# A first stage with twelve channel tiles as float32 products in place of six split ones

## The chip, the cores and the metric

The kernel runs on one core of one Trainium2 chip. The metric is the device time of one execution in microseconds (us); lower is better.

## The reference, cut to what matters

Two blocks follow each other on 256 tokens of 1024 channels, all in float32. The change lies at the start of the first block:

```
shift, scale, gate = adaln(c, w_ada_mix, b_ada_mix)      # silu(c) @ w + b, cut in three
h = rms_norm(x, norm_mix_w) * (1 + scale) + shift
p = h @ w_in                                             # [256, 1024] x [1024, 9248]
a, b = p[:, 0:1024], p[:, 1024:2048]                     # gated input of the convolution branch
u = a * sigmoid(b)                                       # then a causal convolution of 31 taps, a layer
                                                         # norm over the channels, silu, @ w_conv_out
z, xBC, dt, gates = the other columns of p               # state space branch
x = x + gate * (merged branches @ w_out)
```

After it come the feed-forward of the first block and a second block with two mixers (gated delta rule, gated linear attention) and two MLPs. They are not changed.

## The kernel before

Tokens are two tiles of 128. Nearly every weight goes through `w3`: a DMA into a buffer `raw` (six of them), a cast `whi` by ACT and the rest `wlo = raw - whi` by DVE, both in float32r. `whi` and `wlo` share eight buffers, tag "w". A product then is three float32r matmuls (`mm3`, L185 to L187): whi·hi, whi·lo, wlo·hi of the activations `hh`, `hl`. For some items `wlo` is made by a DMA with addition instead (L166, issued by POOL): those with a running number over `NW` that four doesn't divide. The order of the instructions on each engine, and of the DMAs on SP's queue, is written ahead by the program's scheduler from priorities; on the chip each engine follows it and waits where an operand is late.

`start()` makes h. For each k of the eight blocks of 128 input channels it loads two items of `w_ada_mix`, multiplies and sums them against silu(c) on DVE (L399; `g`, that is `self.sc`, holds silu(c) on every partition), adds biases, transposes block k of the normed x (L312), scales and shifts it into `f` (L323), and splits f into `hh` and `hl`. Beside this it already multiplies six channel tiles (three of a, three of b) by item k of `w_abe`, 768 columns. Their six accumulators, [128, 256] each, take half a PSUM bank each: three banks of tag "a", three of tag "b".

`state_space()` turns the three finished pairs into u (`ev_ab`: tanh on ACT L572, product on DVE L573) and starts their convolution taps (`conv_taps`, L490: 30 dependent DVE instructions for each of eight channel tiles, at a priority far behind all else, so that they fill DVE's gaps), then multiplies dt (`small_tok`), the other five pairs from `w_ab` (two items each), B and C (`w_bc`), and the groups of the state space part. `mix_gates` and `merge` follow. In `merge` four pairs i of `w_ssm_out` are multiplied; before the last of them stands `conv_ln`, the layer norm over the channels of the convolution's result `acc`, which makes the operands `ch` and `cl` of the `w_conv_out` products. The first of these products needs all 240 taps.

## Time and profile before

| | us |
|---|---|
| three runs | 1447.05, 1451.47, 1452.64 |
| their median | 1451.47 |
| span of the profiled execution, first to last instruction | 1448.5 |
| PE busy in the span | 1317.5 (91%) |
| DVE busy | 991.1 (68%) |
| ACT busy | 755.5 (52%) |

The profile gives the span of its execution and no separate time for it; the span lies 2.97 us under the median of the three runs. PE is TensorE's matmuls, PEld its weight loads, DVE VectorE, ACT ScalarE, POOL GpSimd, SPq the issuing of DMAs by SyncE. Times in rows are us from the span's start. A matmul's busy time includes its way through the array, so the time that one costs in a dense run is read from start to start.

### The profile page before, as it was taken

To read this page: it belongs to the slowest core of one execution; us is meant where nothing else is said; L and a number is where in the kernel's file an instruction comes from. 1 tells how busy PE (TensorE), PEld (TensorE's weight loads), DVE (VectorE), ACT (ScalarE), POOL (GpSimd) and SP (SyncE) were. 2 spreads that over 40 slices of the span, in tenths; PEclk is the share of its full clock that TensorE was granted. 3 is DMA by queue.
4 is the path that set the end of the run, shared out by engine and by line. 5 is a ranking of instruction groups with operands and counts; after the bars stand their busy time and mean duration, and the time that the engine had idled before them with its cause. 6 is when DMAs were issued, how large, how long until landed. Compare 5 with 4: busy or idle time off the path is not lost. (4 is left out here: it accounts for less than half of the span.)

```text
span 1448.5 us, 21890 instructions
## 1 busy us (share of the span) xinstructions
PE 1317.5 (91%) x8408; PEld 1183.6 (82%) x8408; DVE 991.1 (68%) x1797; ACT 755.5 (52%) x1202; POOL 162.1 (11%) x179
## 2 busy tenths in 40 slices
PE   5899999979999999988768878999998998999997
PEld 4888788879987999978767866799886986788896
DVE  7878898669567664734579975855464796765453
ACT  4667687635446443626695434544443645454350
POOL 0112232210000000012411431000000000000000
PEclk9999999999999999999879999999998999999999
DMA  9899789998266764739468214765354313576430
GB/s 338 280 266 262 193 232 237 289 290 310 83 214 210 248 213 162 252 124 238 108 155 209 88 45 145 256 206 187 136 189 144 117 59 117 173 252 213 156 123 29
DMA packets 75049, 273.33 MB, mean 189 GB/s; under 512 B 8608, under 2 KB 8736, under 8 KB 74433
## 3 DMA queue, kind: packets, MB, share of 16 engines
q1 hardware_dynamic: 62208, 224.08, 44.7%
q0 software_dynamic: 12736, 47.85, 15.9%
q8 instruction: 66, 1.08, 0.3%
q14 instruction: 39, 0.31, 0.1%
HBM read 232.06 MB, written 2.10 MB: 162 GB/s over the span
## 5 line engine op out<-in xcount | busy, mean ns | idle before, releaser
L187 PE MATMUL psa<-hh,wlo 128*128 128x256 f32 x1448 | 420.3, 290 | 24.1 <-DMA wlo<-raw 20.7
L185 PE MATMUL psa<-hh,whi 128*128 128x256 f32 x1448 | 419.6, 290 | 3.7 <-DVE c L490 1.8
L186 PE MATMUL psa<-hl,whi 128*128 128x256 f32 x1448 | 418.0, 289 | 0.8 <-DVE hl L180 0.5
L170 DVE TENSOR_TENSOR wlo<-raw,whi 128x1024 fp32r<-128x1024 f32 (+1 forms) x203 | 244.5, 1211 | 155.3 <-ACT whi L169 148.8
L169 ACT CAST whi<-raw 128x1024 fp32r<-128x1024 f32 (+1 forms) x203 | 210.1, 1040 | 215.0 <-PE psa L186 143.8
L187 PEld LDWEIGHTS psa<-hh,wlo 128*128 128x128 f32 x1448 | 284.5, 196 | 30.7 <-DMA wlo<-raw 25.1
L185 PEld LDWEIGHTS psa<-hh,whi 128*128 128x128 f32 x1448 | 284.9, 197 | 8.0 <-ACT hh L179 2.9
L186 PEld LDWEIGHTS psa<-hl,whi 128*128 128x128 f32 x1448 | 284.3, 196 | 4.0 <-DVE hl L180 1.8
L170 DVE TENSOR_TENSOR xlo<-raw,xhi 128x1024 fp32r<-128x1024 f32 x100 | 121.0, 1221 | 60.9 <-ACT xhi L169 57.1
L169 ACT CAST xhi<-raw 128x1024 fp32r<-128x1024 f32 x100 | 104.8, 1050 | 93.7 <-DMA raw<-in_w_mlp 58.1
L185 PE MATMUL psb<-xhi,hid 128*128 128x512 f32 x344 | 136.1, 395 | 1.6 <-ACT hid L316 1.6
L187 PE MATMUL psb<-xhi,hidl 128*128 128x512 f32 x344 | 136.1, 396 | 0.0
L186 PE MATMUL psb<-xlo,hid 128*128 128x512 f32 x344 | 135.7, 395 | 0.0
L166 POOL DMA_DIRECT2D wlo<-raw x72 | 62.7, 871 | 419.5 <-ACT wlo L165 194.5
L490 DVE SCALAR_TENSOR_TENSOR acc<-u,vecs,acc 128x229 f32<-128x229 f32 (+28 forms) x240 | 105.1, 479 | 0.3
L165 ACT ACTIVATE wlo<-raw 128x1024 fp32r<-128x1024 f32 x72 | 76.2, 1058 | 43.7 <-PE psa L186 30.0
L186 PE MATMUL psa<-wlo,hh 128*128 128x512 f32 x208 | 83.9, 405 | 4.1 <-DVE wlo L170 3.2
L185 PE MATMUL psa<-whi,hh 128*128 128x512 f32 x208 | 85.0, 410 | 1.0 <-ACT hh L179 0.8
L399 DVE CUSTOM_DVE_ANT_0 raw<-raw,g 128x1024 f32<-128x1024 f32 x48 | 58.6, 1220 | 38.8 <-DMA raw<-in_w_ada_ffn 21.6
L187 PE MATMUL psa<-whi,hl 128*128 128x512 f32 x208 | 83.5, 404 | 0.0
L185 PEld LDWEIGHTS psb<-xhi,hid 128*128 128x128 f32 x344 | 64.8, 188 | 15.6 <-ACT hid L316 1.8
L187 PEld LDWEIGHTS psb<-xhi,hidl 128*128 128x128 f32 x344 | 64.7, 188 | 15.0
(388 smaller groups left out, 2234.7 us busy)
## 6 DMA issues: line engine op xcount, KB each, us to landing
raw<-in_w_mlp SPq DMA_DIRECT2D x120, 512.0 KB, 4.1
wlo<-raw POOLq DMA_DIRECT2D x72, 512.0 KB, 7.4
raw<-in_w_ffn_in SPq DMA_DIRECT2D x40, 512.0 KB, 4.3
raw<-in_w_ada_mix SPq DMA_DIRECT2D x24, 512.0 KB, 5.5
raw<-in_w_ada_ffn SPq DMA_DIRECT2D x24, 512.0 KB, 5.1
raw<-in_w_qkv SPq DMA_DIRECT2D x24, 512.0 KB, 5.9
raw<-in_w_ffn_down SPq DMA_DIRECT2D x22, 512.0 KB, 4.3
raw<-in_w_xs SPq DMA_DIRECT2D x16, 512.0 KB, 4.9
```

The lines of the kernel that those rows point to most:

```text
L165: nc.scalar.activation(out=lo, in_=t, func=AF.Copy, scale=-1.0)
L166: nc.gpsimd.dma_start(out=lo, in_=t, accum_op=ALU.add)
L169: nc.scalar.copy(hi, t)
L170: nc.vector.tensor_tensor(out=lo, in0=t, in1=hi.bitcast(F32), op=ALU.subtract)
L185: mm(out, ah, bh, start=start, stop=False)
L186: mm(out, ah, bl, start=False, stop=False)
L187: mm(out, al, bh, start=False, stop=stop)
L399: self.nc.vector.tensor_tensor_reduce(out=w, in0=w, in1=self.sc, scale=1.0, scalar=0.0, op0=ALU.mult, op1=ALU.add, accum_out=mod[:, i : i ...
L490: nc.vector.scalar_tensor_tensor(out=o, in0=i, scalar=taps[:, j : j + 1], in1=o, op0=ALU.mult, op1=ALU.add)
```

## The change

- c is loaded as [128, 8] (`c8`, 4 KB) and not as a broadcast [128, 1024]. Its silu is taken on eight columns, and `rows_of`, the former body of `gate_rows`, spreads it over the partitions: eight diagonal matrices on DVE, eight products with a matrix of ones on TensorE, two copies by ACT. The identity's load moves ahead of x's.
- The first stage makes twelve channel tiles (`NE = 6` pairs). Their weights are used as they arrive, in float32, without a split: one float32 matmul in place of three float32r ones. They are loaded straight into the buffers of tag "w", two pieces of 128 x 768 for each k. Two accumulators share a bank; only the first product of a bank has `start`.
- f of both tiles of tokens is one [128, 256] operand, scaled by one instruction, and is split by one pair of instructions behind the products.
- Two pairs instead of five are left for `w_ab`. The running number is set so that the items from `w_bc` on are split as before.
- The masks' load on POOL's queue keeps its place in the program, behind the first stage. `gate_rows` takes one buffer of tag "f" for four diagonals.

```diff
-NW = 14
+NW = 15
+NE = 6
 def consts(self):
-        self.sc = self.g4()
-        t = self.smt([P, D], "xn")
-        nc.sync.dma_start(self.sc, self.A["c"].broadcast_to([P, D]))
-        nc.scalar.activation(out=t, in_=self.sc, func=AF.Tanh, scale=0.5)
+        self.mod2 = cp.tile([P, 24], F32, name="mod2")
+        self.c8 = self.mod2[:, 0:8]
+        nc.sync.dma_start(self.c8, self.A["c8"])
+        nc.sync.dma_start(self.ident, self.A["masks"][:, 0])
+    def silu_c(self):
+        t = self.mod2[:, 8:16]
+        nc.scalar.activation(out=t, in_=self.c8, func=AF.Tanh, scale=0.5)
         nc.vector.tensor_scalar(out=t, in0=t, scalar1=0.5, scalar2=0.5, op0=ALU.mult, op1=ALU.add)
-        nc.vector.tensor_tensor(out=self.sc, in0=t, in1=self.sc, op=ALU.mult)
+        nc.vector.tensor_tensor(out=t, in0=t, in1=self.c8, op=ALU.mult)
+        self.sc = self.rows_of(t, 1.0)
 def load_consts(self):
-        nc.gpsimd.dma_start(self.mk, self.A["masks"][:, 1:NMASK0])
+        self.tc.keep_in_program_order(nc.gpsimd.dma_start(self.mk, self.A["masks"][:, 1:NMASK0]))
     def gate_rows(self, mod, scale):
+        return self.rows_of(mod[:, 16:24], scale)
+    def rows_of(self, v, scale):
         g = self.g4()
         for hf in range(2):
             b = self.pS()
+            dgs = self.smt([P, 4, P], "f")
             for k4 in range(4):
                 k = hf * 4 + k4
-                dg = self.smt([P, P], "dg")
+                dg = dgs[:, k4]
                 nc.vector.tensor_scalar(
-                    out=dg, in0=self.ident, scalar1=mod[:, 16 + k : 17 + k], scalar2=scale, op0=ALU.mult, op1=ALU.mult
+                    out=dg, in0=self.ident, scalar1=v[:, k : k + 1], scalar2=scale, op0=ALU.mult, op1=ALU.mult
                 )
                 nc.tensor.matmul(b[:, k4 * P : (k4 + 1) * P], self.ones, dg, start=True, stop=True)
             nc.scalar.copy(g[:, hf * 512 : hf * 512 + 512], b)
 def start(self):
-        nc.sync.dma_start(self.ident, A["masks"][:, 0])
+        self.silu_c()
-        banks = [(self.pa(), self.pb()) for i in range(3)]
+        banks = [self.pa() if i % 2 == 0 else self.pb() for i in range(NE)]
         for k in range(8):
...
+            b = self.pS()[:, :T]
             for t in range(2):
-                self.xpose_split(xn[t], t, h[0], h[1], a, mod[:, 0:8], ks=(k,), n=1)
-            wh, wl = self.w3("w_abe", k, 6)
-            for i in range(3):
-                for m in range(2):
-                    self.mm3(
-                        banks[i][m][:, :T], wh[:, 2 * i + m], wl[:, 2 * i + m], h[0][:, :, k], h[1][:, :, k],
-                        k == 0, k == 7,
-                    )
+                nc.tensor.transpose(b[:, t * P : (t + 1) * P], xn[t][:, k * P : (k + 1) * P], self.ident)
+            f = self.smt([P, 4, P], "f").rearrange("p t c -> p (t c)")[:, :T]
+            nc.scalar.activation(out=f, in_=b, func=AF.Identity, scale=a[:, k : k + 1], bias=mod[:, k : k + 1])
+            for e in range(2):
+                w = self.wp.tile([P, 1024], F32, tag="w", bufs=8, name=self.nm("we"))
+                nc.sync.dma_start(w[:, : NE * P], A["w_abe"][2 * k + e])
+                for i in range(NE // 2):
+                    o = banks[e * NE // 2 + i]
+                    for m in range(2):
+                        ins = nc.tensor.matmul(
+                            o[:, m * T : (m + 1) * T], w[:, (2 * i + m) * P : (2 * i + m + 1) * P], f,
+                            start=(k + m == 0), stop=(k == 7), skip_group_check=True,
+                        )
+                        if m > k:
+                            self.tc.keep_in_program_order(ins)
+            f3 = f.rearrange("p (t c) -> p t c", t=2)
+            self.split(h[0][:, :, k], h[1][:, :, k], f3)
+        self.nw = 14
         self.load_consts()
-        self.mod2 = self.cp.tile([P, 24], F32, name="mod2")
 def state_space(self, h, banks):
-        for i in range(3):
-            ev_ab(i)(banks[i][0][:, :T], banks[i][1][:, :T])
+        for i in range(NE):
+            ev_ab(i)(banks[i][:, :T], banks[i][:, T:])
         self.small_tok("w_dt", h, ev_dt)
-        self.projA([("w_ab", i, lambda b, i=i: ev_ab(i + 3)(b[:, :T], b[:, T:])) for i in range(5)], h)
+        self.projA([("w_ab", i, lambda b, i=i: ev_ab(i + NE)(b[:, :T], b[:, T:])) for i in range(8 - NE)], h)
```

`layout()` cuts `w_abe` and `w_ab` to match, and stores `w_abe` as 16 pieces of 128 x 768.

## Rows read from the trace of the kernel before

**Rows 1.** The page: the span and the number of instructions.

```profile
span 1448.5 us, 21890 instructions
```

**Rows 2.** Busy time by stretch: start and end of the stretch, its length, busy us of each engine (instructions), then the granted clock of TensorE, the DMA engines' share and GB/s. The first stage's products run from 16.7 to 46.9, dt to 55.1, the five pairs of `w_ab` to 85.2; the last tap is over at 361, the first product of `w_conv_out` starts at 387.

```profile
0.00:10.00 10.00, 0.00 (x0) 0.00 (x0) 2.08 (x3) 4.17 (x8) 1.31 (x8) 1.00 0.84 281
10.00:20.00 10.00, 4.95 (x19) 4.00 (x20) 9.05 (x23) 4.02 (x12) 1.88 (x2) 1.00 1.00 373
16.70:46.90 30.20, 26.10 (x157) 22.02 (x156) 28.19 (x73) 14.63 (x38) 2.95 (x7) 1.00 0.97 351
46.90:55.10 8.20, 6.42 (x38) 5.88 (x37) 6.48 (x9) 6.98 (x11) 0.00 (x0) 0.79 0.84 298
55.10:85.20 30.10, 29.41 (x243) 29.11 (x243) 29.52 (x79) 20.72 (x32) 6.41 (x7) 1.00 0.89 235
85.20:361.00 275.80, 250.81 (x1717) 231.50 (x1716) 227.10 (x457) 181.16 (x301) 54.07 (x59) 0.95 0.92 260
```

**Rows 3.** The start in order of time: start, length, engine, line, operation, and in brackets the idle time before it and what ended it.

```profile
5.26 1.06 ACT L380 ACTIVATE xn<-g 128x1024 f32<-128x1024 f32 x1 [3.25 <-DMA g<-in_c]
8.17 0.63 ACT L446 ACTIVATE xn<-x 128x512 f32<-128x512 f32 x1 [1.85 <-DMA x<-in_x]
11.31 1.22 DVE L399 CUSTOM_DVE_ANT_0 raw<-raw,g 128x1024 f32<-128x1024 f32 x1
15.48 0.81 ACT L323 ACTIVATE f<-pss,mod,ada_mix 128x128 f32<-128x128 f32 x2 [2.12 <-DVE ada_mix L416]
16.73 0.58 PE L185 MATMUL psa<-hh,whi 128*128 128x256 f32 x1
```

**Rows 4.** One k of the first stage on DVE, in order of time (left out: the second L399 and short operations of L399, L411 and L416).

```profile
28.05 1.22 DVE L399 CUSTOM_DVE_ANT_0 raw<-raw,g 128x1024 f32<-128x1024 f32 x1
...
29.20 0.49 DVE L180 TENSOR_TENSOR hl<-f,hh 128x128 fp32r<-128x128 f32 x2
...
31.16 0.96 DVE L170 TENSOR_TENSOR wlo<-raw,whi 128x768 fp32r<-128x768 f32 x1
32.04 1.22 DVE L399 CUSTOM_DVE_ANT_0 raw<-raw,g 128x1024 f32<-128x1024 f32 x1
```

**Rows 5.** PE in order of time: float32r products early in the first stage, later in it, and at its end and the start of dt.

```profile
17.53 0.41 PE L185 MATMUL psb<-hh,whi 128*128 128x256 f32 x1
17.75 0.41 PE L185 MATMUL psa<-hh,whi 128*128 128x256 f32 x1
...
22.41 0.28 PE L186 MATMUL psa<-hl,whi 128*128 128x256 f32 x1
22.53 0.28 PE L187 MATMUL psa<-hh,wlo 128*128 128x256 f32 x1
...
46.84 0.28 PE L187 MATMUL psb<-hh,wlo 128*128 128x256 f32 x1
48.15 0.38 PE L185 MATMUL pss<-hh,whi 128*128 128x256 f32 x1 [1.03 <-ACT whi L169]
```

**Rows 6.** PE in order of time: float32 products that are not split; a record count of two for each product.

```profile
120.79 0.60 PE L606 MATMUL pss<-bc 128*128 128x256 f32 x2
121.23 0.27 PE L607 MATMUL pss<-bc 128*128 128x128 f32 x1
...
364.62 3.61 PE L780 MATMUL pss<-acc,ones 128*128 128x256 f32 x16
367.89 0.47 PE L185 MATMUL psa<-yT,whi 128*128 128x256 f32 x1
```

**Rows 7.** The evacuations of the first and the last of the five `w_ab` pairs on ACT.

```profile
60.91 0.36 ACT L572 ACTIVATE th<-psa 128x256 f32<-128x256 f32 x1
85.46 0.36 ACT L572 ACTIVATE th<-psa 128x256 f32<-128x256 f32 x1
```

**Rows 8.** DMA issues: queue, times issued, KB each, median us from issue to landing (the first two in the stretch 0 to 47, the last over the whole span).

```profile
raw<-in_w_abe SPq DMA_DIRECT2D x8, 384.0 KB, 5.4
g<-in_c SPq DMA_DIRECT2D x1, 512.0 KB, 4.5
wlo<-raw POOLq DMA_DIRECT2D x72, 512.0 KB, 7.4
```

**Rows 9.** The taps alone (L490 on DVE): busy time in one stretch (columns as in Rows 2, DVE alone), and the last taps in order of time.

```profile
46.90:85.20 38.30, 23.27 (x56) 0.96 0.88 249
...
360.08 0.99 DVE L490 SCALAR_TENSOR_TENSOR acc<-u,vecs,acc 128x254 f32<-128x254 f32 x2
```

**Rows 10.** The longest of DVE's waits from 85 to 361, in total: us, times, longest.

```profile
DVE raw L399 <- DMA raw<-in_w_ada_ffn: 17.1, 8, 6.8
```

**Rows 11.** From `conv_ln` to the first product of `w_conv_out`, in order of time, and the clock in one stretch of it (columns as in Rows 2).

```profile
368.27 0.38 ACT L782 ACTIVATE mu<-pss 128x256 f32<-128x256 f32 x1 [8.28 <-PE pss L780]
379.98 2.49 DVE L812 TENSOR_TENSOR acc<-acc,rb 128x512 f32<-128x512 f32 x4 [0.39 <-ACT rb L808]
387.03 0.28 PE L185 MATMUL psa<-ch,whi 128*128 128x256 f32 x1
...
374.00:376.00 2.00, 2.00 (x12) 2.00 (x11) 0.00 (x0) 0.29 (x1) 0.00 (x0) 0.50 0.00 0
```

**Rows 12.** `gate_rows` before: two of its diagonals on DVE, the copy of half a row on ACT.

```profile
392.07 0.48 DVE L430 TENSOR_SCALAR dg<-ident,mod 128x128 f32<-128x128 f32 x2
602.60 0.59 ACT L434 COPY g<-pss 128x512 f32<-128x512 f32 x1 [1.47 <-PE pss L433]
```

More of the change, by code (lines that the diff above doesn't have):

```diff
@@ L375, in consts @@
         nc.gpsimd.memset(self.mhalf, -0.5)
-        self.sc = self.g4()
-        t = self.smt([P, D], "xn")
-        nc.sync.dma_start(self.sc, self.A["c"].broadcast_to([P, D]))
-        nc.scalar.activation(out=t, in_=self.sc, func=AF.Tanh, scale=0.5)
+        self.mod2 = cp.tile([P, 24], F32, name="mod2")
[3 more added lines that the diff above has]
+    def silu_c(self):
+        nc = self.nc
+        t = self.mod2[:, 8:16]
+        nc.scalar.activation(out=t, in_=self.c8, func=AF.Tanh, scale=0.5)
         nc.vector.tensor_scalar(out=t, in0=t, scalar1=0.5, scalar2=0.5, op0=ALU.mult, op1=ALU.add)
-        nc.vector.tensor_tensor(out=self.sc, in0=t, in1=self.sc, op=ALU.mult)
+        nc.vector.tensor_tensor(out=t, in0=t, in1=self.c8, op=ALU.mult)
+        self.sc = self.rows_of(t, 1.0)
     def load_consts(self):
@@ L1624, in layout @@
     A["x"] = np.ascontiguousarray(f["x"][0].reshape(2, P, D).transpose(1, 0, 2))
-    A["c"] = np.ascontiguousarray(f["c"])
+    A["c8"] = np.ascontiguousarray(_chan(f["c"].reshape(-1)))
     for n in ("w_ada_mix", "w_ada_ffn"):
@@ L1629, in layout @@
     ar = np.arange
-    A["w_ab"] = _chunks_a(w, [o + ar(c, c + P) for c in range(384, D, P) for o in (0, D)])
-    A["w_abe"] = _chunks_down(np.concatenate([w[:, o + c : o + c + P] for c in range(0, 384, P) for o in (0, D)], 1))
+    A["w_ab"] = _chunks_a(w, [o + ar(c, c + P) for c in range(NE * P, D, P) for o in (0, D)])
+    A["w_abe"] = _chunks_down(np.concatenate([w[:, o + c : o + c + P] for c in range(0, NE * P, P) for o in (0, D)], 1))
+    A["w_abe"] = np.ascontiguousarray(A["w_abe"].reshape(8, P, 2, NE * P).transpose(0, 2, 1, 3)).reshape(16, P, NE * P)
     A["w_z"] = _chunks_tok(w, 2048, 4096)
```

## The prediction

> **What bounds the kernel now.** I read the busy time by stretch first, then the stretches around the change in order of time, then the waits, the DMA issues and the end of the convolution. The execution to which everything is summed spans 1448.5 [rows 1]; its median of runs lies 2.97 higher, at 1451.47.
>
> The first stage isn't bound by TensorE: 30.2 us lie between its first product and its last, and the 144 products in them need 17.3 at the later spacing of 0.12 [rows 2, 5]. DVE is busy for 28.2 of the 30.2, with a k every 3.99 us (28.05 to 32.04), and the DMA engines show a share of 0.97 at 351 GB/s: DVE sets the pace and the DMAs are close behind [rows 2, 4]. After it comes dt, 24 products (2.9 us), in 8.2 us: PE waits for the cast of a weight that could not be made sooner, and the clock of the stretch falls to 0.79 [rows 2, 5]. From 55.1 to 85.2 PE is busy for 29.4 of 30.1: here it is the bound, and DVE is full as well (29.5), because the taps fill its gaps [rows 2]. From 85 to 361 PE is busy 91% and DVE 82%. The last tap is done at 361, and `conv_ln` with the first product of `w_conv_out` at 387 hangs on it [rows 2, 9, 11]. So there are two threads: PE's, and the taps on DVE, which have to be through when `merge` comes to its last pair.
>
> **The start.** c lands as 512 KB, ahead of x, and the masks' 320 KB (five blocks of 128 x 128) travel beside x [rows 8]. Both leave the way: 0.85 MB at 351 GB/s are 2.4 us; the identity, now ahead of x, gives 0.2 back. x was there at 8.17 and the first product started 8.56 later [rows 3]. It no longer needs the cast of h: f was ready at 16.29, the product came at 16.73, which saves 0.44. So 16.73 - 2.2 - 0.4 = 14.1. The new path of c must not be later: silu on eight columns (some 0.8 us with its hops, an estimate), eight diagonals at 0.24 each, eight float32 products of 128 columns at half of 0.44, doubled for the low clock, 3.5 us, and a copy of 0.59 behind the last [rows 6, 12]; overlapped about 5 us after c8 lands. If c8 lands at 3, the rows are there at 8.0, before DVE needs them near 8.7 (11.31 less 2.6); if it lands at 5.2 as the 512 KB did, at 10.2, 1.5 late [rows 3]. I take nothing and keep 1.5 for the range.
>
> **The stage.** It now has 12 products for each k, 96 in all, in plain float32. The trace of before has such products elsewhere: sixteen records for eight products from 364.62 to 367.89, 0.41 each, and 0.44 for one at 120.79 [rows 6]. I take 0.43; the split triple that it replaces is 3 x 0.12 = 0.36. Two transposes for each k add at most 0.12 each, 1.9. At first the spacing of products was 0.21, twice the later one, for 5.6 us (16.7 to 22.3), although the clock's column says 1.00 there: that is the level of 1.2 GHz against 2.4 [rows 2, 5]. I keep 5.6 us, in which 6.5 products are made. So the stage ends at 14.1 + 5.6 + 89.5 x 0.43 + 1.9 = 60.1, against 46.9 before; 58.3 with 0.41, 61.0 with 0.44. This is PE's own pace, 5.4 us for a k. The others keep up: DVE loses the weights' rest (0.96) and stands at about 3.1 for a k; ACT loses the weights' cast; the DMAs have 1.84 MB for a k, 4.9 us at 373 GB/s [rows 2, 4]. If that cover fails, the DMA rival below applies.
>
> **dt and the pairs.** While PE works off the stage, the weights of dt and of the first two pairs' items can be loaded and split ahead, since the buffers of tag "w" come free with every k. So dt costs its 2.9 and 0.3 for the transposes, not 8.2: 63.3. Two pairs in place of five: 96 products at 0.12, 11.5. Three of the four items get their rest by a DMA with addition, which takes 7.4 us to land [rows 8]; for the last two it starts only when their buffers are freed (60 and 63) and lands about as they are due, so I add 0.7. The pairs end at 75.5. Before, they ended at 85.2 (the last evacuation is at 85.46, four pairs after that at 60.91) [rows 7]. PE's thread is 9.7 us ahead. The six evacuations at the stage's end are no wait: three start 2.6 us before it, and the banks that the pairs need come free first.
>
> The masks' load moves behind the stage on POOL's queue. Behind it there stand only the scalings of the vectors; it lands well before dt's sums near 63, so it costs nothing; without that cover it would cost its flight, bounded by the 7.4 of that queue [rows 8]. The shared buffer of `gate_rows` is used twice later, for which 0 to 1 us each is the bound, and I take 0. From `w_bc` on the items are split as before, so PE's order and waits there stay the same and the lead should travel along.
>
> **The taps.** They don't get shorter with the pairs. From 46.9 to 85.2 DVE did 56 taps in 23.3 us, 0.42 each [rows 9]. In the new kernel the time from the first evacuation (about 58.5) to the end of the pairs is 17 us, of which 3.3 go to the eight evacuations, 2.3 to two weight rests and 3.3 to dt's chain: room for 8.1 us, 20 taps. So up to 36 taps, about 14.5 us, are pushed behind, and nothing that DVE was spared (the rests of six items of the pairs, the stage's) lies where they then have to go. Below, the bound is 0: DVE idles for 48.7 us from 85 to 361, and at least 17.1 of them are waits for the weights of the modulation, which taps put ahead of them would fill [rows 2, 10]. But the order is written ahead, and the taps run right up to 361, so the gaps of the chip are gaps that the order doesn't know. I take 10. The last tap then falls at 361 - 9.7 + 10 = 361.3.
>
> From the last tap to the first product of `w_conv_out` it took 26.0 us, with the 96 products of the last pair of `w_ssm_out` (11.5) in PE's way; without them it would be some 14.5 [rows 11]. PE's thread would reach that product at 387.0 - 9.7 = 377.3. With 14.5 the taps hold it up only if they are more than 11.5 late; with 26.0 all of their lateness is lost. For 10 late the loss lies between 0 and 10, and a PE that has waited starts at the low clock, as the 0.50 at 374 shows for this place [rows 11]. I take 2.5, near the lower end, because the pair's products can be over before the last tap.
>
> **Sum.** -9.7 + 2.5 = -7.2: a span of 1441.3, and with the 2.97 a time of 1444.3. A measurement of this kernel can tell about 0.5% (7.3 us) from no change, so the forecast sits on that line.
>
> **Rivals.**
> *The whole lead stays* (or more: weights of `w_conv_out` split while PE waits): -9.7 to -12, 1440 to 1442. For it: the idle 48.7 us of DVE [rows 2]. Against it: the taps reach to 361 [rows 9].
> *The taps become the bound* (the slower side). Place: `conv_ln`. If all 36 come behind and the chain takes its 26.0 us again, the product comes at 361 - 9.7 + 14.5 + 26.0 = 391.8, 4.8 later than before, and with up to 2.8 for the low clock 7.6: 1456 to 1459. It decides from a lateness of 9.7 on, with the long chain; a shorter chain gives -2 and more.
> *The stage hangs on its DMAs.* It must load 15.8 MB by its end. It ends by DMA at 2 + 15.8 / rate + 2.6, which passes 60.1 below 285 GB/s; at the 298 of the stretch after the stage nothing is lost, at the 249 of 46.9 to 85.2 it is 8 us: 1452 [rows 2, 9]. For it: 281 in the first 10 us. Against it: 351 over the whole stage and 373 at its best, with pieces of 384 and 512 KB and several of them under way [rows 2, 8]. The Trainium skill (DMA: Bandwidth & Descriptors, Bandwidth) asks for 1 MB in a transfer and gives 138 GB/s for 64 KB and 341 for 1 MB; by an estimate of 250 between the two the stage would end 8 us later and most of the lead would be gone. The trace disagrees with that rule: its 373 was reached with pieces of at most half that size.
> *The clock stays low in the stage*: 96 x 0.86 in place of 43, 38 us more, 1482. The dense float32 rows elsewhere run at 0.41 [rows 6], so this is remote.
>
> **Chances.** Forecast case, -4 to -9.7 (its own range 1442 to 1447.5): 0.45. Whole lead: 0.20. Taps the bound, with every degree from -4 to +8: 0.17. DMAs: 0.08. Clock and unforeseen order effects on both sides: 0.10. Faster by over 0.5%: half of the first, all of the second, 0.03 of the rest, 0.45. Slower by over 0.5%: 0.05 of the taps, 0.02 of the DMAs, 0.04 of the last, 0.11. Within: 0.44. The range reaches from the whole lead with the quicker product (1437) to the taps with the long chain (1457).
>
> **What would show it.** In the new profile: the first products near 14; 96 pairs of records at 0.21 to 0.22 with PE at 10 of 10 until about 60; dt without a gap; the second `w_ab` evacuation near 75.5; the last tap and the first `ch` product against 361 and 387, and whether PE idles between. The forecast is wrong if the stage ends after 65, or if PE stands still before `w_conv_out` for over 5 us.

## The result, and the profile after

| | before | after |
|---|---|---|
| median of six runs each, on one chip, us | 1448.98 | 1459.64 |
| span of the profiled execution, us | 1448.5 | 1456.6 |

The changed kernel is slower: the ratio is 1.0074, with a 95% interval of 1.0051 to 1.0097, some 10.7 us of 1449. Forecast were 1444.3 and a range up to 1457; slower by over 0.5% had a chance of 0.11. What is accounted for below are the 8.1 us by which the two profiled executions differ (the page answers to [rows 1]).

The page of the changed kernel, the span:

```profile
span 1456.6 us, 21668 instructions
```

Busy time by stretch of the changed kernel (columns as in [rows 2]): up to the first product, the first stage, dt with the two pairs of `w_ab`, from there to the last tap; the last row is the stretch 46.9 to 62.6 alone.

```profile
0.00:15.18 15.18, 5.10 (x21) 4.07 (x21) 6.48 (x23) 5.61 (x14) 2.21 (x9) 1.00 0.84 321
15.18:62.60 47.42, 46.11 (x205) 39.58 (x206) 25.72 (x64) 10.91 (x23) 3.90 (x7) 1.00 0.83 318
62.60:82.70 20.10, 17.66 (x131) 16.95 (x129) 15.70 (x49) 15.77 (x24) 4.39 (x5) 0.92 0.93 245
82.70:378.70 296.00, 257.47 (x1772) 236.99 (x1771) 242.50 (x488) 182.56 (x307) 55.63 (x60) 0.95 0.89 247
46.90:62.60 15.70, 15.26 (x74) 13.22 (x73) 7.29 (x20) 5.69 (x12) 2.83 (x6) 1.00 0.42 144
```

The stage is now PE's (46.1 of 47.4 us busy), as forecast. The fourth row is the one that matters: to its last tap DVE needs 242.5 us of work and stands idle for 53.5, where before it was 227.1 and 48.7 in 85.2 to 361 [rows 2]. The last row shows a hole that the forecast didn't have: the DMA engines are busy for 0.42 of the stage's last 15.7 us. The kernel before has 0.80 in the same 15.7 us, which there lie behind the stage:

```profile
46.90:62.60 15.70, 13.92 (x100) 13.34 (x100) 13.40 (x29) 11.04 (x17) 0.97 (x1) 0.89 0.80 275
```

What the loads wait for stands in the changed kernel's SyncE queue from 40 to 63: a buffer of tag "raw", of which there are six, and at the end the one that dt's weight holds until its rest is made (L172).

```profile
SPq L153 <- DVE wlo L172: 8.5, 1, 8.5
```

The start and the stage in order of time, in the changed kernel (columns as in [rows 3]); the last three lines are one of the stage's short stops.

```profile
6.87 0.63 ACT L460 ACTIVATE xn<-x 128x512 f32<-128x512 f32 x1 [4.32 <-DMA x<-in_x]
10.40 1.22 DVE L408 CUSTOM_DVE_ANT_0 raw<-raw,g 128x1024 f32<-128x1024 f32 x1
14.56 0.56 ACT L546 ACTIVATE f<-pss,mod,ada_mix 128x256 f32<-128x256 f32 x1 [4.17 <-PE pss L544]
15.18 1.65 PE L553 MATMUL psa<-f,we 128*128 128x256 f32 x3 [0.44 <-ACT f L546]
...
28.30 0.38 PE L544 MATMUL pss<-ident,xn 128*128 128x128 f32 x2
28.50 0.56 ACT L546 ACTIVATE f<-pss,mod,ada_mix 128x256 f32<-128x256 f32 x1 [8.53 <-PE pss L544]
29.12 0.48 PE L553 MATMUL psa<-f,we 128*128 128x256 f32 x1 [0.44 <-ACT f L546]
```

dt and the two pairs, on ACT, DVE and PE: the cast of dt's weight behind the stage's first evacuations (`th`), the rests of two weights, PE's wait for a rest that comes by DMA, and the tanh of the two last pairs (the answer to [rows 7]).

```profile
58.47 0.38 ACT L596 ACTIVATE th<-psa 128x256 f32<-128x256 f32 x1 [2.65 <-PE psa L553]
60.16 1.03 ACT L171 CAST whi<-raw 128x1024 fp32r<-128x1024 f32 x1
61.91 2.35 DVE L172 TENSOR_TENSOR wlo<-raw,whi 128x1024 fp32r<-128x1024 f32 x2
71.94 0.58 PE L189 MATMUL psa<-hh,wlo 128*128 128x256 f32 x1 [2.44 <-DMA wlo<-raw]
76.17 0.39 ACT L596 ACTIVATE th<-psa 128x256 f32<-128x256 f32 x1 [4.33 <-PE psa L189]
82.90 0.38 ACT L596 ACTIVATE th<-psa 128x256 f32<-128x256 f32 x1
```

The pairs end at 82.9, not at 75.5: 2.6 us ahead of before, not 9.7. Next, what DVE waits for most between 82.7 and 378.7 (the answer to [rows 10]), two single waits in front of a product and sum for the modulation (the profile names no releaser for the first), and PE behind the second of them:

```profile
DVE raw L408 <- DMA raw<-in_w_ada_ffn: 17.9, 8, 6.0
...
110.52 1.22 DVE L408 CUSTOM_DVE_ANT_0 raw<-raw,g 128x1024 f32<-128x1024 f32 x1 [10.15 <-issue]
265.87 1.23 DVE L408 CUSTOM_DVE_ANT_0 raw<-raw,g 128x1024 f32<-128x1024 f32 x1 [4.66 <-DMA raw<-in_w_ada_ffn]
267.76 0.48 PE L699 MATMUL psb<-xdt,E 128*128 128x64 f32 x1 [4.07 <-DVE E L694]
```

And `conv_ln`, which answers to [rows 9] and [rows 11]: the sums over the taps' results on PE, the last taps on DVE, mu, the first product of `w_conv_out`.

```profile
369.01 2.75 PE L804 MATMUL pss<-acc,ones 128*128 128x256 f32 x12
372.20 0.70 PE L804 MATMUL pss<-acc,ones 128*128 128x256 f32 x2 [0.43 <-DVE acc L504]
375.09 3.57 DVE L504 SCALAR_TENSOR_TENSOR acc<-u,vecs,acc 128x249 f32<-128x249 f32 x7
378.71 1.22 PE L804 MATMUL pss<-acc,ones 128*128 128x256 f32 x2 [4.75 <-DVE acc L504]
379.97 0.38 ACT L806 ACTIVATE mu<-pss 128x256 f32<-128x256 f32 x1 [15.59 <-PE pss L804]
395.96 0.40 PE L187 MATMUL psa<-ch,whi 128*128 128x256 f32 x2
```

Before, the sixteen records of these sums ran in one piece from 364.62, without a wait for DVE [rows 6]. Now the last two wait 4.75 us for the last tap, and the two ahead of them 0.43. The first product of `w_conv_out` comes at 395.96, 8.9 us later than before [rows 11]; the rest of the kernel is of the same length.

The loss can be written as one line of DVE's: it enters the stretch 2.5 us earlier (82.7 for 85.2), has 15.3 us more to do and 4.8 us more idle time, so its last tap ends 17.6 us later, at 378.7; from there to the first product of `w_conv_out` it takes 17.3 us and not 26.0, which gives 8.7 back.

### The profile page after: what moved, and what is told of

Read it like the earlier page. It is cut to its first block, busy times and chain, and to the rows that moved or that the text cites. A ratio compares the mean times of both kernels' runs of the same rounds, so it can differ in the third digit from the quotient of the medians.

```text
span 1456.6 us, 21668 instructions
## 1 busy us (share of the span) xinstructions
PE 1321.8 (91%) x8328; PEld 1183.6 (81%) x8328; DVE 978.4 (67%) x1784; ACT 740.4 (51%) x1173; POOL 161.2 (11%) x178
## 5 line engine op out<-in xcount | busy, mean ns | idle before, releaser
L189 PE MATMUL psa<-hh,wlo 128*128 128x256 f32 x1376 | 398.9, 290 | 28.5 <-DMA wlo<-raw 26.3
L187 PE MATMUL psa<-hh,whi 128*128 128x256 f32 x1376 | 398.0, 289 | 4.1 <-DVE c L504 3.7
L188 PE MATMUL psa<-hl,whi 128*128 128x256 f32 x1376 | 396.4, 288 | 0.0
L172 DVE TENSOR_TENSOR wlo<-raw,whi 128x1024 fp32r<-128x1024 f32 x190 | 231.5, 1225 | 166.2 <-ACT whi L171 154.5
L171 ACT CAST whi<-raw 128x1024 fp32r<-128x1024 f32 x190 | 198.3, 1049 | 223.2 <-PE psa L188 149.7
L189 PEld LDWEIGHTS psa<-hh,wlo 128*128 128x128 f32 x1376 | 270.0, 196 | 34.3 <-DMA wlo<-raw 30.2
L187 PEld LDWEIGHTS psa<-hh,whi 128*128 128x128 f32 x1376 | 270.2, 196 | 7.0 <-issue 4.1
L188 PEld LDWEIGHTS psa<-hl,whi 128*128 128x128 f32 x1376 | 270.0, 196 | 2.3 <-issue 0.2
L172 DVE TENSOR_TENSOR xlo<-raw,xhi 128x1024 fp32r<-128x1024 f32 x100 | 121.2, 1222 | 53.6 <-ACT xhi L171 51.9
L504 DVE SCALAR_TENSOR_TENSOR acc<-u,vecs,acc 128x227 f32<-128x227 f32 (+26 forms) x240 | 108.5, 493 | 1.1 <-ACT acc L497 0.7
L167 ACT ACTIVATE wlo<-raw 128x1024 fp32r<-128x1024 f32 x71 | 75.2, 1059 | 34.7 <-PE psa L188 20.1
L188 PE MATMUL psa<-wlo,hh 128*128 128x512 f32 x208 | 85.9, 415 | 7.5 <-DMA wlo<-raw 5.2
L187 PE MATMUL psa<-whi,hh 128*128 128x512 f32 x208 | 86.1, 416 | 1.5 <-ACT hh L181 0.8
L189 PE MATMUL psa<-whi,hl 128*128 128x512 f32 x208 | 84.8, 410 | 0.0
L187 PEld LDWEIGHTS psb<-xhi,hid 128*128 128x128 f32 x344 | 64.8, 188 | 15.7 <-ACT hid L318 2.1
L189 PEld LDWEIGHTS psb<-xhi,hidl 128*128 128x128 f32 x344 | 64.7, 188 | 15.4 <-DVE hidl L182 0.3
```

The source lines that it names most:

```text
L167: nc.scalar.activation(out=lo, in_=t, func=AF.Copy, scale=-1.0)
L171: nc.scalar.copy(hi, t)
L172: nc.vector.tensor_tensor(out=lo, in0=t, in1=hi.bitcast(F32), op=ALU.subtract)
L187: mm(out, ah, bh, start=start, stop=False)
L188: mm(out, ah, bl, start=False, stop=False)
L189: mm(out, al, bh, start=False, stop=stop)
```

## The experiments

Three theories were set against each other. **T**: the taps on DVE come too late for `conv_ln`. **L**: PE's lead is eaten because weights come no earlier. **O** was formed after ne4: the program's scheduler, called the planner here, writes each engine's order from its own estimates, and the change made it write another order for code that was not touched. In the labels b_ stands for the kernel before, a_ for the changed one, ne4 for the changed one with four pairs in the first stage. From the first instruction of `w_bc` to the last of `merge` both kernels issue the same instructions (the taps aside); on DVE 75 of 289 stand in another place, on ACT 117 of 332, on PE 338 of 1958, on GpSimd 10 of 63, and SyncE's loads in the same.

All ratios are against the kernel before on the same chip; the runs were made on several chips, so two of them are compared by their ratios. The other columns come from one profiled execution of each, in us: the last u of `w_ab` (the pairs are done), the first tanh of `w_g` (tg, between the state space part and `merge`), the end of the last tap, the first product of `w_conv_out` (ch). In the runs with eight taps the last tap is early and not listed.

| kernel | ratio, 95% interval | last u | first tg | last tap | first ch |
|---|---|---|---|---|---|
| before | 1 | 85.9 | 271.8 | 361.1 | 387.0 |
| after | 1.0074 (1.0051 to 1.0097) | 83.4 | 277.9 | 378.7 | 396.0 |
| b_taps | 1.0048 (1.0027 to 1.0068) | 86.1 | 280.8 | | 394.9 |
| a_taps | 1.0004 (0.9985 to 1.0022) | 82.4 | 273.8 | | 386.7 |
| b_noload | 1.0043 (1.0025 to 1.0061) | 85.1 | 282.2 | 360.4 | 391.6 |
| a_noload | 0.9935 (0.9914 to 0.9956) | 82.1 | 269.5 | 360.3 | 380.6 |
| a_ada0 | 1.0095 (1.0057 to 1.0132) | 84.6 | 275.4 | 379.1 | 398.7 |
| b_ada0 | 1.0003 (0.9982 to 1.0024) | 85.2 | 276.2 | 360.0 | 387.1 |
| b_c8 | 1.0014 (0.9990 to 1.0037) | 82.9 | 269.5 | 357.2 | 384.5 |
| ne4 | 1.0087 (1.0057 to 1.0117) | 84.1 | 280.4 | 371.5 | 393.9 |
| a_ord | 1.0028 (1.0008 to 1.0048) | 83.6 | 275.3 | 371.1 | 390.6 |
| b_aord | 1.0027 (1.0009 to 1.0045) | 85.7 | 280.1 | 362.1 | 391.0 |
| ne4_ord | 0.9993 (0.9970 to 1.0016) | 81.9 | 266.2 | 358.2 | 379.1 |
| a_nw19_ord | 1.0051 (1.0031 to 1.0070) | 78.2 | 272.0 | 371.7 | 389.9 |
| a_ordx | 1.0054 (1.0035 to 1.0074) | 84.8 | 271.8 | 373.6 | 394.8 |
| a_nw19_ordx | 1.0047 (1.0021 to 1.0072) | 79.1 | 264.9 | 368.4 | 386.8 |
| a_ord_taps | 1.0000 (0.9989 to 1.0010) | 81.8 | 273.3 | | 387.4 |
| b_ord_taps | 0.9966 (0.9950 to 0.9982) | 84.3 | 265.6 | | 378.6 |
| a_nw19_ordx_taps | 0.9936 (0.9914 to 0.9957) | 77.7 | 260.8 | | 371.7 |
| ne4_nw19_ord | 1.0024 (1.0004 to 1.0045) | 83.9 | 269.0 | 366.0 | 389.9 |

### Fewer taps, and no loads of the modulation, in both kernels

```diff
 def conv_taps(self, out, src, taps, bias, ntap, pad):
-        for j in range(ntap):
+        for j in range(max(0, ntap - 8), ntap):
```

Expected of b_taps:

> The kernel before with the wide convolution cut from 31 taps to its last 8 (8 x 23 = 184 DVE instructions left out, some 75 us of DVE work; the output changes for it). Its partner is a_taps. Theory T (taps): after loses because the taps on DVE come too late for conv_ln. Theory L (loads): it loses because PE's lead is eaten by weights that come no earlier, the DMA engines being idle for over half of the stretch 46.9 to 62.6 and near full from there on. Here neither theory gives much: PE is busy from 361 to 387 before, so a tap less frees no PE time there. Both expect 0 to 12 us less than before (1437 to 1449), from waits between 85 and 361.

Expected of a_taps:

> The changed kernel with the same cut of the taps to 8. To be set against b_taps. Theory T: with the taps gone the whole loss goes, and what is left of the lead shows: a_taps 2 to 10 us faster than b_taps, the first product of w_conv_out earlier than in b_taps. Theory L: the taps made only the last 4.6 us of the loss (the step between the second and the third evacuation of merge, +5.08 to +9.67); a_taps stays 3 to 6 us slower than b_taps.

```diff
 def ada(self, name, i, mod, load=True):    # load=False for the columns that wait
-        w = self.raw(self.A[name][i])
+        w, v = (a buffer of tag "raw", not loaded), self.sc
         self.nc.vector.tensor_tensor_reduce(
-            out=w, in0=w, in1=self.sc, ...
+            out=w, in0=v, in1=self.sc, ...
```

Expected of b_noload:

> The kernel before without the loads of the 24 columns of the modulation that wait behind the first stage (w_ada_ffn, and w_ada_mix 16 to 23): DVE does the same 24 products and sums, on silu(c) twice, and the buffer is taken as before; 12.6 MB of loads are left out, about 37 us of the DMA engines at 340 GB/s (the output changes for it). Partner of a_noload. Both theories: 5 to 25 us faster than before, since DVE's 17.1 us of waits for those loads go.

Expected of a_noload:

> The changed kernel without the same loads, against b_noload. Theory L: with the DMA engines relieved PE's lead is not eaten: the evacuations of w_bc, w_xs and w_g stay 2 us or more ahead of b_noload's up to the first tg, and a_noload is at most 3 us slower than b_noload and more probably faster. Theory T: the loads don't matter, the taps are as late as before, and a_noload stays 8 to 11 us slower than b_noload.

With few taps the changed kernel beats its partner by 0.44%, without loads by 1.1%. So T got its sign on the first pair and L on the second; T missed the second (8 to 11 us slower was expected of it), L the first. The two don't exclude each other: without the loads the last tap of the changed kernel came at 360.3 and not at 378.7, where T expected it as late as before, since DVE's idle time up to there fell from 53.5 us to 38.6. What nobody expected: the kernel *before* became 0.5% slower when 75 us of DVE's work were left out, and 0.4% slower without 12.6 MB of loads. Less work and more time can't be the work; the order is new in both (for the taps this is tested below, for b_noload it was not). Here is the column of the modulation that stands ahead of E on DVE, in b_taps and, below, in the kernel before (where another one had waited 3.32 us at 255.44, ahead of xdt):

```profile
268.44 1.23 DVE L399 CUSTOM_DVE_ANT_0 raw<-raw,g 128x1024 f32<-128x1024 f32 x1 [10.03 <-DMA raw<-in_w_ada_ffn]
...
262.39 1.22 DVE L399 CUSTOM_DVE_ANT_0 raw<-raw,g 128x1024 f32<-128x1024 f32 x1 [1.06 <-DMA raw<-in_w_ada_ffn]
```

It is the place (ahead of E, between the last xsT, the group's input on DVE, and the first tg) at which a column waited 4.66 us in the changed kernel.

### The wait at the first item of w_g, one part alone, and a shorter stage

```diff
-            self.ada_next(ADA_PER[1])
+            self.ada_next(ADA_PER[1] if i else 0)
```

Expected of a_ada0:

> The changed kernel without the two columns of the modulation beside the first item of w_g; they are made two later, all columns are still made. Theory L, made sharper: of the loss 7.9 us arise between the last product of group 3 (2 us ahead at 258) and the first tg (6.1 us behind at 278), because in the new order of DVE these two columns stand ahead of E <- E of the group, wait 4.66 us for their loads, and PE waits 4.07 us for E. With them gone the first tg comes 5 to 9 us earlier (269 to 273) and the time falls by 4 to 8 us to 1452 to 1456. Theory T: the last tap (378.7) sets the end whatever PE's thread does; 1457 to 1461.

Expected of b_ada0:

> The control of a_ada0: the same edit in the kernel before, whose columns at this place waited only 1.06 us. Theory L: -2 to +2 us (1447 to 1451), the first tg within 2 us of 271.8. If it moves by more than 4 us either way, any new order of DVE is worth as much as the whole difference, and neither theory is needed for it.

The stretch from the last xsT to the first tg fell to 19.6 us (28.3 in the changed kernel), but the new order had lost 6.2 us by the last xsT (255.8 for 249.6), so the first tg came only 2.5 us sooner, and the time did not fall: the last tap ended at 379.1 and PE waited 4.90 us for it, as T says. The control moved by 4.4 us at the first tg, over the 4 us set for it, and by nothing at the end: a first sign of what an order does. L in this sharpened form, which expected 4 to 8 us less, is refuted as the cause of the time.

The start alone, in the kernel before (`consts`, `silu_c`, `rows_of` and the masks' load as in the change), and then the change with a shorter stage:

```diff
-NE = 6
+NE = 4
-        self.nw = 14
+        self.nw = 10
```

Expected of b_c8:

> One part alone: the kernel before with c loaded as 4 KB and spread by TensorE, the identity ahead of x and the masks behind the stage; the first stage as before, six tiles of split weights. DVE's order behind the stage is that of before word for word. Both theories: the first product 1 to 1.5 us earlier than at 16.73; L expects that 0.85 MB less in front of the weights stay as a lead of 1 to 2 us to the end (1447 to 1448.5), T expects the same, as the taps come earlier by as much.

Expected of ne4:

> The changed kernel with eight channel tiles in the first stage instead of twelve (4 pairs; the running number set so that w_bc on are split as in both). PE then needs 8 x 0.43 + 0.24 = 3.7 us for a k, the DMAs 1.57 MB, 3.9 us at 406 GB/s, DVE about 3.1: the stage should end near 50 and leave the DMA engines no hole at its end. Theory L: the DMA share in the 15 us ahead of the stage's end stays over 0.8, the pairs end 2 to 6 us ahead of 85.2, and the time is 1443 to 1452, between 8 and 16 us under the changed kernel. Theory T: taps start at 48 instead of 59, so of the 18 that are still to do at 361 in the changed kernel about 10 go, 4 us; 1453 to 1457.

The start's lead of 2.5 us in the profiled execution stayed up to the first ch with the old order; in the median of the runs it can't be seen. ne4 was no faster than the changed kernel, 8 to 16 us were expected by L and at least 2.6 by T: both missed, which led to O. In its profile the sums over the taps ran in one piece from 371.51, right behind the last tap (371.47) and without a wait of PE, so late taps alone can't be its loss.

### The order of the untouched stretch, exchanged

```diff
+ORDER = {"DVE": ..., "Activation": ..., "Pool": ..., "PE": ...}    # places in the other kernel
 def state_space(self, h, banks):
+        self.mark = len(self.nc.cur_bb.bb.instructions)
         bc = self.bigt([P, 8, T], name="bc")
 def merge(self, yT, acc, tg):
+        self.pin()    # ahead of gate_rows: each instruction since mark, but for the taps, behind
+                      # the one that precedes it in ORDER, by an edge without a semaphore
```

Expected of a_ord:

> The changed kernel, with the instructions from the first of w_bc to the last of merge (DVE 289, ACT 332, GpSimd 63, PE 1958; the 240 taps stay free) pinned on each engine to the order that they have in the kernel before; the loads have that order already. Theory O (order): the change made the planner write a new order for this stretch, and that order costs 8 to 10 us; with the old order the stretch from the first bc to the first product of w_conv_out takes 285.7 us as before, the lead of 2.4 to 3.5 us stays, and the time is 1443 to 1449. Theory T (taps): the taps are still behind (12 instructions at every milestone instead of 26), they hold up the sums of conv_ln; 1452 to 1458.

Expected of b_aord:

> The counterpart: the kernel before, its start and its pairs untouched, with the same stretch pinned to the order of the changed kernel. Theory O: it takes over the loss, first product of w_conv_out at 395 to 400 instead of 387, 1456 to 1463. Theory T: its taps start as early as before, so that little is lost; 1447 to 1452.

Expected of ne4_ord:

> Eight channel tiles in the first stage (as ne4), and the stretch behind the pairs in the order of the kernel before. Theory O: ne4's 1461 falls to 1445 to 1450. Theory T: the last tap, 371.5 in ne4, moves by a few us only; 1452 to 1458.

The old order takes 0.46% off the changed kernel, the new one puts 0.27% on the kernel before, and ne4 falls by 0.94% to the time of before (1446.8 us, in O's range; its last tap moved by 13.3 us, where T expected a few). Here is the new order's wait in b_aord, whose start, pairs and taps are those of before:

```profile
267.71 1.23 DVE L409 CUSTOM_DVE_ANT_0 raw<-raw,g 128x1024 f32<-128x1024 f32 x1 [4.05 <-DMA raw<-in_w_ada_ffn]
269.60 1.97 PE L686 MATMUL psb<-xdt,E 128*128 128x64 f32 x8 [3.11 <-DVE E L681]
```

O's direction holds, its size doesn't: a_ord was to be at 1443 to 1449 and came at 1452.9, in T's 1452 to 1458, and b_aord, with 1456 to 1463 expected, at 1453.8. The order is a part, not the whole.

### Where the old order and the lead end

Here bc are the evacuated results of `w_bc`. Two edits, alone and together: the rests of all `w_ab` items by DVE, and the pinning from the first of `w_xs` on instead of `w_bc`.

```diff
-NW = 15
+NW = 19
...
-        self.mark = len(self.nc.cur_bb.bb.instructions)
         bc = self.bigt([P, 8, T], name="bc")
...
+        self.mark = len(self.nc.cur_bb.bb.instructions)
         yT = []
```

Expected of a_nw19_ord:

> a_ord, and in addition the rests of the three w_ab items that come by a DMA with addition made by DVE (three instructions of 1.2 us), since PE waited 2.44 us at 71.94 for one of them and the pairs ended at 82.7 where 75.5 was forecast. Theory O: pairs end 2 to 4 us sooner than in a_ord and the lead travels: 1440 to 1446. Theory T: DVE gets 3.7 us more work in front of the taps, no faster than a_ord.

Expected of a_ordx:

> As a_ord, but pinned only from the first of w_xs on; w_bc's part is left to the planner as in the changed kernel. In a_ord the first bc came at 107.6 (101.3 before, 97.8 in the changed kernel), because the old order puts the first sums over dt ahead of the casts of w_bc, and dt's chain on DVE ends at 83 there. Theory O: with that artefact gone the first bc is back near 98, the second near 113.7, the rest takes before's time: first product of w_conv_out at 384 to 388, 1446 to 1451, at least 2 us under a_ord. If it stays at 1452 or more, the order of w_bc's part was not what a_ord lost by, and taps or loads are left.

Expected of a_nw19_ordx:

> a_ordx with the rests of all w_ab items by DVE. In a_nw19_ord the pairs ended 7.6 us ahead of before (78.2), nearly the lead that the prediction gave them, and the lead was gone at the first bc. Theory O: with w_bc's part free at least 3 us of it reach the first product of w_conv_out (381 to 385), 1442 to 1448. Theory L (weights come no earlier than before): the second bc comes at 112 to 115 all the same, as the load of the first w_ada_ffn column is issued behind w_xs and lands near 111; no more than 1 us better than a_ordx.

a_nw19_ord was no faster than a_ord, as T said: its pairs ended 5.4 us sooner, its last tap 0.6 us later. In a_ordx the first bc was back at 98.8, but the time was 1457.3 where O expected 1446 to 1451. Its PE thread is back where the kernel before had it (first tg at 271.8, second evacuation of `merge` at 357.2 against 357.9), and yet the first ch comes only 1.2 us sooner than in the changed kernel, because of this:

```profile
363.64 3.18 PE L830 MATMUL pss<-acc,ones 128*128 128x256 f32 x14
373.67 1.22 PE L830 MATMUL pss<-acc,ones 128*128 128x256 f32 x2 [6.85 <-DVE acc L514]
```

In a_nw19_ordx the lead travels, against L, which expected the second bc at 112 to 115 (it came at 104.6): pairs done 6.8 us ahead, first tg 6.9, the second evacuation of `merge` 8.0 (349.9 against 357.9). In time it gained nothing clear of noise (1.0047 after 1.0054), and O's 1442 to 1448 was missed, because it all ends at the same place:

```profile
264.92 0.58 ACT L752 ACTIVATE tg<-psa 128x512 f32<-128x512 f32 x1
...
357.63 1.46 PE L830 MATMUL pss<-acc,ones 128*128 128x256 f32 x6
361.31 1.04 PE L830 MATMUL pss<-acc,ones 128*128 128x256 f32 x2 [2.23 <-DVE acc L514]
368.46 1.22 PE L830 MATMUL pss<-acc,ones 128*128 128x256 f32 x2 [6.11 <-DVE acc L514]
...
386.81 0.28 PE L197 MATMUL psa<-ch,whi 128*128 128x256 f32 x1
```

Pairs 6.8 us earlier, last tap 7.3 us later, first ch at the same time as before. Set against their partners, the two runs with `NW = 19` also show what the rests by DMA cost at the stage's end: 5.4 and 5.7 us of the pairs. What DVE does from the end of the pairs to the last tap, in a_ord, a_ordx, a_nw19_ordx and b_aord (one view of each kernel, DVE alone):

```profile
82.90:371.10 288.20, 240.93 (x487) 0.96 0.91 254
```

```profile
84.10:373.60 289.50, 242.67 (x488) 0.96 0.89 251
```

```profile
78.40:368.40 290.00, 244.79 (x502) 0.96 0.88 250
```

```profile
85.00:362.10 277.10, 224.84 (x454) 0.96 0.92 255
```

The work is 241 to 245 us wherever the stage makes twelve tiles, and 225 to 227 where it makes six. The idle time is 45 to 49 us with the old order (48.7 before) and 52 to 54 with the new one (52.3 here in b_aord, 53.5 in the changed kernel); ne4, for which the planner wrote an order of its own, has 56.0. So the new order costs DVE 4 to 6 us, and the stage costs it about 15 us of work.

### The same without most taps

Expected of a_ord_taps:

> a_ord with the wide convolution cut to its last 8 taps: 184 DVE instructions, some 75 us, left out, every other instruction in the same order (the output changes for it). Theory T: what is lost by taps goes; in a_ord the sums of conv_ln end with the last tap (371.1, mu at 371.9), so 3 to 8 us faster than a_ord, and faster than b_ord_taps by its lead. Against T: within 2 us of a_ord.

Expected of b_ord_taps:

> The kernel before with the same cut of the taps and its own order pinned (the run b_taps had a new order, 8.5 us longer between the last xsT and the first tg). Theory O: b_taps was slower than before by its order alone, so with the old order it is 1444 to 1450, 6 us or more under b_taps. In before the last tap ends 3.6 us ahead of the sums, so the taps themselves are worth 0 to 5 us. If it stays near 1455, orders explain nothing.

Expected of a_nw19_ordx_taps:

> a_nw19_ordx with the wide convolution cut to its last 8 taps (the output changes for it). In a_nw19_ordx the lead of 7 to 8 us did travel (first tg 264.9 against 271.8, second evacuation of merge 349.9 against 357.9) and ended at conv_ln: PE waited 2.23 and 6.11 us for the taps, the first product of w_conv_out came at 386.8. Theory T: without those taps it comes at 376 to 381, 6 to 10 us earlier than in a_nw19_ordx, and the time falls by 5 us or more to 1444 to 1450. Theory L (PE's thread itself is held by loads): no more than 3 us.

b_ord_taps against b_taps, the same instructions in two orders: 0.9966 and 1.0048, 11.8 us by order alone. Where b_taps waited 10.03 us for a load, b_ord_taps waits this long:

```profile
255.58 1.23 DVE L409 CUSTOM_DVE_ANT_0 raw<-raw,g 128x1024 f32<-128x1024 f32 x1 [1.71 <-DMA raw<-in_w_ada_ffn]
```

b_ord_taps is also the control for the other two. In the kernel before no sum waited for a tap, and still the cut takes 0.34% off it and brings its first ch 8.4 us forward, since 75 us of work less on DVE moves other things too (the first tg by 6.2 us).

a_ord_taps is 0.28% under a_ord, as T expected, but that is no more than the control. With all taps a_ord is 0.28% behind before, with eight 0.34% behind b_ord_taps, so late taps are not what a_ord lost by; in its trace PE waits 0.27 us for the last one. In a_ord the old order sets the casts of `w_bc` behind the first sums over dt, and dt's chain ends at 83 there; in a_ord_taps the first bc comes at 105.3, in b_ord_taps at 99.7.

a_nw19_ordx_taps decides for the version without that artefact. Without the taps its sums run in one piece, the first ch comes 15.1 us sooner than in a_nw19_ordx (6 to 10 were expected; 4.1 of them are there at the first tg), and the time falls by 1.1%, about three times as much as the control.

```profile
351.62 3.61 PE L830 MATMUL pss<-acc,ones 128*128 128x256 f32 x16
371.74 0.28 PE L197 MATMUL psa<-ch,whi 128*128 128x256 f32 x1
```

With all taps this version is 0.47% behind the kernel before, with eight it is 0.3% ahead of b_ord_taps: the taps turn the sign, as in the first pair, where the planner was free. With few taps, and rests by DVE, the change does what the forecast wanted of it.

For the changed kernel itself this leaves two causes, both shown at work: the new order (with the old one its last tap comes 7.6 us and its first ch 5.4 us sooner, a_ord) and the taps' work that the longer stage pushes behind. How much of the 10.7 us is each was not separated, since the pinned order brought a loss of its own.

Expected of ne4_nw19_ord:

> A candidate for a version that beats both: ne4_ord with all rests of the eight w_ab items by DVE instead of four of them by a DMA with addition (PE waited 3.3 us in four pieces for such rests). Theory L: pairs end 1 to 3 us sooner, 1443 to 1447. Theory T: DVE is full from 55 to 82 as before (20.1 of 20.1 us in ne4_ord), so the rests push 10 taps behind and the last tap, at 358.2 with 0.5 us of slack, comes 3 to 5 us later; 1447 to 1452.

It came in T's range, and 4 us behind ne4_ord: the rests on DVE put taps behind (the last one 7.8 us later, 3 to 5 were expected), and the sums waited 1.85 us at 366.05. No version here that computes the same beats the kernel before; ne4_ord beats the changed one by 0.8% and equals before.

One thing stays open in part. In a_nw19_ordx the first ch is at the time of before, but the kernel is 0.47% slower. Behind the mixer PE issues the same products in the same order as in a_ord, whose length from there to the end is that of before within 1 us; in the profiled execution of a_nw19_ordx that part took 8.5 us longer. The trace shows where more than half of it arises: stretches in which TensorE fell to the lower of its two clock levels, 1.2 for 2.4 GHz. Here are the same products in a_ord and, below, in a_nw19_ordx (columns as in [rows 2]):

```profile
799.69:806.79 7.10, 5.97 (x51) 5.62 (x49) 6.17 (x13) 3.62 (x10) 2.56 (x4) 1.00 0.00 0
928.40:931.40 3.00, 3.00 (x18) 2.66 (x19) 3.00 (x6) 2.75 (x5) 0.00 (x0) 1.00 0.85 306
...
798.00:808.03 10.03, 7.89 (x49) 7.18 (x50) 9.09 (x15) 5.11 (x11) 4.63 (x4) 0.86 0.12 22
930.55:935.20 4.65, 4.64 (x19) 4.12 (x20) 3.44 (x7) 3.06 (x6) 0.00 (x0) 0.63 0.62 215
```

That is 4.6 us in two stretches, at a granted clock of 0.86 and 0.63 where a_ord has 1.00. Ahead of the second one PE had waited 3.25 us, in a_ord 1.94. Whether the other executions of a_nw19_ordx lose their time in the same way isn't recorded.

## Why the prediction was wrong, step by step

Two steps failed that carry the result. The cover for dt and the pairs didn't hold: PE's thread was 2.5 us ahead at their end and not 9.7 (2.5 of the missing 7.2 us fell in the start and the stage, 4.7 in dt and the pairs). And the taps were taken to be 10 us late, with a last tap at 361.3 and a loss of 2.5 at `conv_ln`; the last tap came at 378.7, 17.6 us later than before, and the loss was 11.4. In order of time:

**What bounds the kernel now** named two threads, and that was right. The reading of where they meet was not. It said that `conv_ln` hangs on the last tap. In the kernel before it hung on PE: the sums started at 364.62, 3.6 us behind the last tap (361.1), and they ran in one piece, without a wait for DVE [rows 6]. From there it follows that the 26.0 us were not a chain from the last tap. Such a chain is 17.3 us long in the changed kernel, and 18.4 to 21.2 in a_nw19_ordx, a_ord and a_ordx.

**The start**: 15.18 for 14.1. x landed 1.3 us sooner, not 2.2; the new path of c was on time for DVE, whose first product and sum came at 10.40 for 11.31, and cost nothing, as taken. f then waited for PE's transposes and started at 14.56, 0.9 us sooner than before. The masks' load went out at 13.43, ahead of the stage's products and not behind the stage.

**The stage**: end at about 62.6 for 60.1. Spacing of 0.43 per product and PE at the bound were right. Missing were the 1.1 us from the start and three stops of 0.44 us (29.12 is one), where the transposes stand just ahead of the products that need their f; together they are the 2.5 us, within 0.1. The rival with the DMAs did not come: 377 GB/s up to 46.9 and 407 in 10 to 40, with weights in pieces of 384 and 512 KB, several under way. The Trainium skill (DMA: Bandwidth & Descriptors, Bandwidth) asks for 1 MB or more in a transfer and gives 341 GB/s for 1 MB, measured on transfers that GpSimd issues; the trace, with smaller pieces issued by SyncE, disagrees.

**dt and the pairs**: the first large error, 20.1 us (62.6 to 82.7) for 15.4; with the 2.5 from before it makes 7.2 of lead. It took dt's 2.9 us and 0.7 for the rests, on the cover that weights are loaded and split ahead while PE works off the stage. They were loaded, but not split. dt's load went out at 41.63, and the two buffers of tag "w" that its split takes were those of the fifth k, whose products were over near 46; so the buffers came free with every k, as the prediction says. What held the cast of dt's weight to 60.16 was its place in ACT's order, behind two evacuations of the stage: ACT stood idle for 2.65 us up to 58.47, waiting for the first of them. In the kernel before it is the same: the cast at 47.06, which the prediction read as one that could not be made sooner, stands behind evacuations at 45.85 and 46.78.

```profile
46.78 0.38 ACT L572 ACTIVATE th<-psb 128x256 f32<-128x256 f32 x1 [0.55 <-DVE u L573]
47.06 1.04 ACT L169 CAST whi<-raw 128x1024 fp32r<-128x1024 f32 x1
```

The rests of dt's weight and of the first `w_ab` item followed on DVE at 61.91, the other three by DMA, beside six evacuations on ACT; PE waited 2.44 us at 71.94 for one of these and then ran at the doubled spacing, 0.21 us, up to 74.7. The rests by DMA are what cost most: with them on DVE the pairs ended at 78 to 79.

**"From `w_bc` on PE's order and waits there stay the same and the lead should travel along"**: the second error. The instructions stay the same, the order doesn't. In front of the last group DVE was 2.2 us ahead (its g, near 257) and PE 0.6 (its product with g, at 258), and at the first tg PE was 6.1 us behind, because a column of the modulation had come to stand ahead of E on DVE. With the old order and the rests on DVE the lead did travel, 8 us of it.

**The taps**: "up to 36 taps, 14.5 us, pushed behind" came out within a microsecond, DVE having 15.3 us more to do, but with some luck. Only 28 more taps were left at the end of the pairs (212 for 184), since the pairs ended late, but all that were left took 96.7 us on DVE for 81.8; and 36 taps at the prediction's own 0.42 would have been 15.1. "I take 10" was wrong, since it let the idle 48.7 us take some of them. Those are waits at the head of an ordered queue, 17.1 us of them for the loads of `w_ada_ffn` alone [rows 10] (17.9 in the changed kernel); at 265.87 DVE stands 4.66 us in such a wait with taps still to do, and does none. The idle time didn't shrink, it grew by 4.8. So the last tap came at 378.7 for 361.3.

**The loss of 2.5 at `conv_ln`** was 11.4: 2.5 us ahead at the end of the pairs, 8.9 behind at the first ch (a part of it came earlier, but in a_ordx, where the first tg is back at the time of before, the first ch comes only 1.2 us sooner). The rival *The taps become the bound* is what happened. It gave 391.8 for the first ch; with the lead measured (+7.2), the longer idle time (+4.8), the work (+0.8) and the shorter chain (-8.7) it gives 395.9. That 391.8 itself lies near the measured 396.0 is in part luck, as these errors of +12.8 and -8.7 nearly cancel. Its chance was too low, and the range's end of 1457 left out the 1459 that it reached with its own price for the low clock. The mark set for a wrong forecast, PE standing still before `w_conv_out` for over 5 us, came as 5.2 us (0.43 and 4.75).

## What to carry to other kernels

When work is moved from one engine's bound to another's, add up the engine that fills its gaps with background work over the whole stretch up to the point where that work is due: entry time plus work plus idle time. Take the idle time as fixed unless a row shows that what fills it may pass the wait, or the wait itself is taken away, as in a_noload. Where a planner writes the order, a local edit changes the order of code it doesn't touch; pinning the old order by edges is a cheap way to separate the two, and a removal experiment without it can have the wrong sign.

## What the runs showed of the hardware

Unexpected was how much an order is worth with the same instructions: 11.8 us between b_taps and b_ord_taps, from a queue in which one wait for a load (10.03 us in the one, 1.71 in the other) holds everything behind it. And the DMA engines can stand idle while loads are still to come: a share of 0.42 in the last 15.7 us of a stage in which they had reached 407 GB/s, because the next load's buffer was not yet read (SyncE's queue waited 8.5 us for one).
